# Dilated heads of a hybrid encoder layer: the first and last query block share a unit with 192 keys each

## The chip, the core and the metric

The kernel runs on one core of a Trainium2 chip. The metric is the device time of one execution in microseconds (us), as the median of several. Engines are named as in the profile: PE is the matrix engine (PEld its loading of the stationary operand), DVE the vector engine, ACT the scalar engine, POOL GpSimd, SP the engine that issues most DMAs.

## The reference

One encoder layer on 1024 tokens of width 1024 in float32: a feed-forward half step, a mixing step with 16 attention heads of width 64, and a second feed-forward half step. Eight heads (group B) mix three dilated windows; this case is about them.

```python
DIL_PATTERNS = ((128, 1), (512, 4), (2048, 16))
...
def dilated_window_attention(q, k, v, t5_bias, window, dilation):
    radius = window // (2 * dilation)
    ...
    off = k_pos[:, None, :] - q_pos[:, :, None]
    valid = (jnp.abs(off) <= radius) & (k_pos[:, None, :] >= 0) & (k_pos[:, None, :] < L)
    bias = t5_bias[:, t5_bucket(off * dilation)].astype(jnp.float32)
    s = jnp.einsum('bhdnqe,bhdnke->bhdnqk', qs, k_blk) * HEAD_DIM ** -0.5
    s = jnp.where(valid, s + bias[:, None], MASK_VALUE)
    m = jnp.max(s, axis=-1, keepdims=True)
    p = jnp.exp(s - m)
    den = jnp.sum(p, axis=-1)
    o = jnp.einsum('bhdnqk,bhdnke->bhdnqe', p, v_blk) / den[..., None]
    lse = m[..., 0] + jnp.log(den)
    ...
def dilated_mixture_attention(q, k, v, t5_bias):
    results = [dilated_window_attention(q, k, v, t5_bias, w, d) for w, d in DIL_PATTERNS]
    wts = jax.nn.softmax(lses, axis=0)
    return jnp.sum(wts[..., None] * outs, axis=0).astype(q.dtype)
```

For the pattern (128, 1), the local one, a query sees the keys at most 64 tokens away. A block of 128 queries in the middle of the sequence so sees 256 keys; the first block (tokens 0 to 127) and the last (896 to 1023) see 192, since there are no tokens beyond the ends.

## The kernel before, in words

The feed-forward steps and the projections come first (to about 890 us), then the eight dilated heads (about 890 to 1012 us), then the eight neighbourhood heads (`na_head`, to about 1120 us), the output projection and the second feed-forward step.

The dilated heads are taken in pairs (class `DilPair`, p = 4 to 7), two heads of 64 columns side by side. A head is 8 units, each with two query blocks: four units for the local part (`part` 0) and four for the dilated part (`part` 1), in two quads of two units. `head` runs the dilated quads first, then the local ones; in the very first head it is the other way round, and its first local quad is begun earlier, among the last products of the projection (`begin`).

A unit goes through these steps. PE makes the scores of each of the two blocks in two products (L1163; the stationary operand is the queries in the tile `st`, the moving one the keys, split into a high and a low part, so two products add up in PSUM). DVE adds the bias and takes the row maximum (`softmax_rows`, L1070), ACT takes the exponential and the row sum (L1072) and writes it in another order of keys. PE transposes the result in blocks of 128 keys (`transpose_blocks`, L1080), ACT or DVE copies it out of PSUM (L1082), and PE multiplies by the values (`outs`, L1184). After two units, one copy brings four blocks of output from PSUM to SBUF (L1192). The values of the local part lie in the tile `va` in slots of 128 tokens, shifted by 64 so that slots blk - 1 and blk serve block blk; the first and the last block have two slots of their own (7, 8 and 9, 10), and their 256 keys are clamped to the ends (`k0`, 0 and 768).

The steps are pipelined by hand: `Ctx.unit` queues a unit's transposes and value products and emits those of three and of four units earlier, so PE sees scores, transposes and value products of three different units in turn. The order is fixed as written for the engines within `ordered`; DMA issues and some POOL work are tied to places by `behind` and `queued`. `next_ready` converts the queries and reorders a bias table on POOL (L1059) for the next head; `merge` joins the patterns after a pair, with two products on POOL (L1237, L1238). Loads of the next heads go through SP (`va` L1100, `vb` L1098, keys L1052, bias L1112) and POOL (queries L1050). In the last two pairs, a quarter of a weight tile is split on ACT and DVE (L127, L128) once per quad.

Of the kernel before, what the change touches and what calls it, by code (L numbers as in the profile page):

```python
# [18 lines left out]
SEQ, D, DFF = 1024, 1024, 2816  # L19
P, T = 128, 512  # L20
# [1054 lines left out]
def transpose_blocks(c, src, n, eng):  # L1075

    nc = c.nc
    ps = c.pst.tile([P, 4, P], F32, tag="tr", name="ptp")
    for j in range(n):
        nc.tensor.transpose(ps[:, j, :], src[:, j * P:(j + 1) * P], c.ident)  # L1080
    pt = c.ptp.tile([P, 4, P], F32, tag="pt", name="pt")
    (nc.scalar.copy if eng else nc.vector.tensor_copy)(pt[:, :n], ps[:, :n])  # L1082
    return pt


class DilPair:


    def __init__(self, c, p, then):

        self.c, self.p, self.pi, self.then = c, p, p - NP, then
        nc, pi = c.nc, self.pi
        vp = c.vp[p % 2]
        self.va = vp.tile([P, 11, P], F32, tag="va", name="va", bufs=1)
        self.vb = vp.tile([P, 4, 2, P], F32, tag="vb", name="vb", bufs=1)
        v = c.v[1][:, pi * P:(pi + 1) * P]
        for j in range(2):
            nc.sync.dma_start(self.vb[:, :, j], v[j * T:j * T + T].rearrange("(i c) f -> i c f", c=4))  # L1098
        for u0, n, t0 in ((0, 7, 64), (7, 2, 0), (9, 2, 768)):
            nc.sync.dma_start(self.va[:, u0:u0 + n], v[t0:t0 + n * P].rearrange("(u t) f -> t u f", t=P))  # L1100

    def outputs(self):
        c = self.c
        self.oa = c.op.tile([P, 8, P], F32, tag="oa", name="oa")
        if self.pi:
            self.sa = c.op.tile([P, 8, 4], F32, tag="sa", name="sa")
        self.ob = c.op.tile([P, 8, RW], F32, tag="ob", name="ob")
# [20 lines left out]
    def quad(self, hd, st, q, g, part, quad, first=False, mid=()):  # L1128
        c, nc = self.c, self.c.nc
        po = []  # L1130
        by_c, g0 = st.rearrange("p q (c t) -> p q c t", c=4), g[:, 0].rearrange("p (c t) -> p c t", c=4)
        for un in range(2):
            if mid and un == mid[1]:
                c.behind(mid[0].popleft(), DVE, ACT)
            if first:
                ps, s, pb = [x.rearrange("p (a b) -> p a b", a=2) for x in (
                    c.psm.tile([P, T], F32, tag="mm", name="sp"), c.sp.tile([P, T], F32, tag="s1", name="s"),
                    c.next_pb())]
            else:
                ps = c.pss.tile([P, 2, 256], F32, tag="s", name="sp")  # L1140
                s = c.pp.tile([P, 2, 256], F32, tag="s", name="s")
                pb = s if part else c.next_pb().rearrange("p (a b) -> p a b", a=2)
            todo = []
            for j in range(2):
                blk = quad * 4 + un * 2 + j
                out, sj = ps[:, j], s[:, j]
                ex = pj = sj
                if part:
                    ci, jh = blk // 2, blk % 2
                    lhs = q[:, blk * P:(blk + 1) * P]  # L1150
                    keys = [st[:, i, ci * 256:(ci + 1) * 256] for i in (1, 2)]
                    bias = g[:, 1, 128 - 128 * jh:384 - 128 * jh]
                else:
                    k0 = min(max(blk * P - 64, 0), 768)
                    lhs = st[:, 0, blk * P:(blk + 1) * P]
                    keys = [by_c[:, i, :, k0 // 4:k0 // 4 + 64] for i in (1, 2)]
                    x0 = k0 - blk * P + 128
                    bias = g0[:, :, x0 // 4:x0 // 4 + 64]
                    ex = sj.rearrange("p (c u t) -> p u c t", c=4, u=2)
                    pj = pb[:, j].rearrange("p (u t c) -> p u c t", u=2, c=4)  # L1160
                    out, sj = [x.rearrange("p (c t) -> p c t", c=4) for x in (out, sj)]
                for i in range(2):
                    nc.tensor.matmul(out, lhs, keys[i], start=i == 0, stop=i == 1)  # L1163
                stt, o0 = (self.ob, P) if part else (self.sa, 0)
                at = blk % 2 * 4 + blk // 2 if part else blk
                todo.append((out, bias, sj, ex, pj, stt[:, at, o0 + hd:o0 + hd + 1],
                             stt[:, at, o0 + 2 + hd:o0 + 3 + hd]))
            for args in todo:
                softmax_rows(c, *args)
            pt, on_act = [], un if part else not (un or quad or first)  # L1170
            c.unit(lambda s=pb, un=un, pt=pt, on_act=on_act: pt.append(
                       transpose_blocks(c, s.rearrange("p a b -> p (a b)"), 4, on_act)),
                   lambda un=un, pt=pt: self.outs(hd, part, quad, un, pt[0], po))

    def outs(self, hd, part, quad, un, pt, po):
        c, nc = self.c, self.c.nc
        if un == 0:
            po.append(c.pso.tile([P, 4, P], F32, tag="o", name="po"))
        po = po[0]
        for j in range(2):  # L1180
            blk = quad * 4 + un * 2 + j
            for t in range(2):
                rhs = self.vb[:, blk // 2, t, :] if part else self.va[:, {0: 7, 7: 9}.get(blk, blk - 1) + t, :]
                nc.tensor.matmul(po[:, un * 2 + j], pt[:, 2 * j + t, :], rhs, start=t == 0, stop=t == 1)  # L1184
        if un == 0:
            return
        f = slice(hd * 64, hd * 64 + 64)
        to, got = self.oa[:, quad * 4:quad * 4 + 4, f], po[:, :, f]
        if part:
            to = self.ob.rearrange("p (j c) w -> p c j w", j=2)[:, 2 * quad:2 * quad + 2, :, f]  # L1190
            got = got.rearrange("p (c j) w -> p c j w", j=2)
        (nc.scalar.copy if quad else nc.vector.tensor_copy)(to, got)  # L1192
        if hd and part:
            self.regroup(quad)
        c.tick()
        if (hd, part, quad) == (1, 0, 1):
            c.todo.extend([lambda: None] + [lambda: c.behind(self.merge, DVE, ACT)])
# [67 lines left out]
def na_head(c, p, hd, og, vs, st, nb, late, done):  # L1265
    nc = c.nc
    kv = [st[:, 1 + i].rearrange("p (r w) -> p r w", r=16) for i in range(2)]
    for s in range(8):
# [24 lines left out]
        def outs(s=s, u=u, k0=k0, n=n, pt=pt, stt=stt, po=po):  # L1293
# [720 lines left out]
```

## Time and profile before

| what | value |
|---|---|
| median of 3 runs | 1832.79 us (1831.18 to 1834.72) |
| profiled execution, its span (the only time that the page gives for it) | 1831.5 us |
| PE busy | 1814.0 us, 99% of the span, 8904 matmuls |
| loading of stationary operands (PEld) | 1526.9 us, 83% |
| DVE, ACT, POOL busy | 1321.9, 835.6, 322.5 us |
| chain that ended last | PE 80%, issue 11%, DMA 3%, DVE 3%, ACT 2%, POOL 1% |

A matmul's busy time is its own duration, and several are under way at once, so busy time on PE is more than the time that PE's work takes; the steps between starts, as the chain shows them, tell what one costs. A float32 value product is recorded as two matmuls, a score product (in the rounded kind, F32R) and a transpose as one.

### The profile page before, as it was taken

How to read it: one execution, taken by the hardware profiler on the slowest of the kernel's cores; microseconds unless marked ns; L12 is line 12 of the kernel's file. 1: busy time of each engine (PE TensorE's matmuls, PEld its weight loads, DVE VectorE, ACT ScalarE, POOL GpSimd, SP SyncE). 2: the span in 40 equal slices, each digit the busy share in tenths (PEclk: the TensorE clock that was granted, in tenths of full speed). 3: DMA queues.
4: the chain of work that ended last, by engine and by line, in shares of the span. 5: the costliest groups of instructions: out<-in, count | busy, mean ns of one | idle time of the engine just before them, and what ended most of it. 6: DMA issues, size and time to landing. Idle time of an engine off the chain costs nothing.

```text
span 1831.5 us, 25146 instructions
## 1 busy us (share of the span) xinstructions
PE 1814.0 (99%) x8904; PEld 1526.9 (83%) x8904; DVE 1321.9 (72%) x2251; ACT 835.6 (46%) x1487; POOL 322.5 (18%) x508
## 2 busy tenths in 40 slices
PE   8999999999999999999999999999999999999998
PEld 6887888888888888888899998888888888888886
DVE  6878876776466877477778866788887777654557
ACT  6622233334443657134688765564223333354433
POOL 2223211112021123132332100121111111110000
PEclk9999999999999999999999999999999999999999
DMA  7756565557888867869686533594555566596564
GB/s 276 260 186 209 163 235 213 212 201 254 307 302 309 280 207 257 271 221 300 199 275 220 196 112 105 183 319 171 187 175 207 191 223 224 184 349 201 189 229 147
DMA packets 172992, 409.67 MB, mean 224 GB/s; under 512 B 20081, under 2 KB 42513, under 8 KB 170818
## 3 DMA queue, kind: packets, MB, share of 16 engines
q1 hardware_dynamic: 124706, 246.33, 40.8%
q0 software_dynamic: 47152, 159.64, 24.0%
q10 hardware_dynamic: 1008, 2.10, 0.3%
q8 instruction: 70, 1.15, 0.3%
q14 instruction: 56, 0.46, 0.1%
HBM read 280.49 MB, written 132.56 MB: 226 GB/s over the span
## 4 chain that ended last, share of the span: by engine, by line
PE 80%; issue 11%; DMA 3%; DVE 3%; ACT 2%; POOL 1%; SPq 0%; POOLq 0%; DVEq 0%; ACTq 0%
PE accp L783 24%; PE mmp L466 14%; PE mmp L467 14%; PE mmp L472 14%; PE po L1184 3%; PE ptp L1080 2%; PE po L1297 2%; PE accp L357 1%; PE accp L359 1%; PE accp L358 1%; PE sp L1163 1%; PE trp L174 1%; PE sp L1281 1%; POOL g L717 1%; ACT pb L1072 1%
## 5 line engine op out<-in xcount | busy, mean ns | idle before, releaser
L466 PE MATMUL mmp<-x,whi 128*128 128x512 f32 (+1 forms) x1464 | 571.8, 391 | 1.6 <-ACT x L181 1.4
L467 PE MATMUL mmp<-x,whi 128*128 128x512 f32 (+1 forms) x1464 | 569.3, 389 | 0.7 <-DVE x L182 0.6
L783 PE MATMUL accp<-pw 128*128 128x512 f32 x1800 | 411.2, 390 | 0.3 <-ACT hb L804 0.3
L783 PEld LDWEIGHTS accp<-pw 128*128 128x128 f32 x1800 | 337.2, 188 | 70.5 <-ACT hb L804 0.7
L472 PE MATMUL mmp<-x,wlo 128*128 128x512 f32 (+1 forms) x1464 | 390.6, 389 | 0.0
L466 PEld LDWEIGHTS mmp<-x,whi 128*128 128x128 f32 x1464 | 275.9, 188 | 59.9 <-ACT x L181 2.0
L467 PEld LDWEIGHTS mmp<-x,whi 128*128 128x128 f32 x1464 | 275.9, 188 | 57.5 <-DVE x L182 1.5
L472 PEld LDWEIGHTS mmp<-x,wlo 128*128 128x128 f32 x1464 | 274.8, 188 | 56.7
L751 DVE TENSOR_TENSOR pw<-praw,pw 128x1024 fp32r<-128x1024 f32 (+1 forms) x181 | 199.6, 1141 | 127.4 <-ACT pw L750 126.7
L750 ACT CAST pw<-praw 128x1024 fp32r<-128x1024 f32 (+1 forms) x181 | 168.4, 983 | 207.1 <-PE accp L783 163.8
L456 ACT CAST whi<-wraw 128x1024 fp32r<-128x1024 f32 x126 | 132.7, 1053 | 186.1 <-PE mmp L467 160.8
L457 DVE TENSOR_TENSOR wlo<-wraw,whi 128x1024 fp32r<-128x1024 f32 x126 | 153.1, 1217 | 2.3 <-ACT whi L456 2.3
L693 POOL DMA_DIRECT2D g<-sg x44 | 24.0, 545 | 432.3 <-DVE sg L686 242.9
L481 ACT COPY s<-mmp 128x512 f32<-128x512 f32 x52 | 30.7, 590 | 132.3 <-PE mmp L472 121.6
L456 ACT CAST whi<-traw 128x512 fp32r<-128x512 f32 x52 | 32.3, 621 | 125.5 <-DVE traw L554 96.4
L645 DVE TENSOR_TENSOR c<-mmp,u 128x512 f32<-128x512 f32 x52 | 35.9, 691 | 70.1 <-PE mmp L472 69.7
L553 DVE TENSOR_TENSOR wraw<-wraw 128x1024 f32<-128x1024 f32 x52 | 63.6, 1224 | 18.5 <-DMA wraw<-in_wu_dram 17.8
L783 PE MATMUL accp<-pw,x 128*128 128x512 f32 x312 | 71.8, 390 | 0.0
L783 PEld LDWEIGHTS accp<-pw,x 128*128 128x128 f32 x312 | 58.3, 188 | 12.3 <-DVE pw L751 0.4
L632 DVE TENSOR_TENSOR c<-mmp,v 128x512 f32<-128x512 f32 x52 | 35.8, 689 | 34.1 <-PE mmp L472 34.1
L1297 PE MATMUL po<-vs,pt 128*128 128x128 f32 x352 | 49.9, 276 | 0.0
L1080 PE MATMUL ptp<-ident,pb 128*128 128x128 f32 x304 | 48.8, 272 | 0.0
(273 smaller groups left out, 2491.4 us busy)
## 6 DMA issues: line engine op xcount, KB each, us to landing
praw<-g SPq DMA_DIRECT2D x70, 512.0 KB, 5.6
wraw<-in_wg_dram SPq DMA_DIRECT2D x44, 512.0 KB, 4.2
wraw<-in_wu_dram SPq DMA_DIRECT2D x44, 512.0 KB, 7.1
tr<-in_wd_dram SPq DMA_DIRECT2D x44, 512.0 KB, 6.3
g<-sg POOLq DMA_DIRECT2D x88, 256.0 KB, 5.4
ts<-tr POOLq DMA_DIRECT2D x22, 1024.0 KB, 4.7
praw<-ts SPq DMA_DIRECT2D x88, 256.0 KB, 3.9
praw<-in_wd_dram SPq DMA_DIRECT2D x66, 256.0 KB, 5.7
```

The costliest lines, as they stand in the source:

```text
L456: nc.scalar.copy(hi, raw)
L457: nc.vector.tensor_sub(lo, raw, hi.bitcast(F32))
L466: mm(out, hi[:, i, sl], xhi[:, k, cols], start=not go_on and k == 0, stop=False, skip_group_check=go_on)
L467: mm(out, hi[:, i, sl], xlo[:, k, cols], start=False, stop=False, skip_group_check=go_on)
L472: mm(out, lo[:, i, sl], xhi[:, k, cols], start=False, stop=k == 3, skip_group_check=go_on)
L553: nc.vector.tensor_sub(r[:, 0:2], r[:, 1:3], r[:, 0:2])
L750: nc.scalar.copy(hi, raw[:, :m])
L751: nc.vector.tensor_sub(lo, raw[:, :m], hi.bitcast(F32))
L783: c.nc.tensor.matmul(acc[t], a, b, start=not chained and gi == 0 and j == i == 0, stop=end and j + n >= len(ops) and i == len(two) - 1, sk ...
L1080: nc.tensor.transpose(ps[:, j, :], src[:, j * P:(j + 1) * P], c.ident)
L1184: nc.tensor.matmul(po[:, un * 2 + j], pt[:, 2 * j + t, :], rhs, start=t == 0, stop=t == 1)
L1297: nc.tensor.matmul(po[0][:, u], pt[0][:, j, :], vs[:, k0 + j, :], start=j == 0, stop=j == n - 1)
```

## The change

Blocks 0 and 7 form a unit of their own, the first one of the second local quad; the other blocks are regrouped: (1, 2) and (5, 6) in the first quad, (0, 7) and (3, 4) in the second. In the edge unit each block has its 192 keys alone, so scores, bias, maximum and exponential run over 2 x 192 columns instead of 2 x 256, and the 384 columns make three transposes. The middle one holds the last 64 keys of block 0 and the first 64 keys of block 7. It is multiplied by two slots of values at once (8 and 9), of which each has 64 tokens and zeros in the other half of the partitions, into the output of both blocks; the other two transposes have a product each. The three products write only the 64 columns of the head at hand. The value tile is loaded with five DMAs instead of three, and POOL clears the two halves that no DMA writes.

```diff
@@ DilPair.__init__
-        for u0, n, t0 in ((0, 7, 64), (7, 2, 0), (9, 2, 768)):
+        for u0, n, t0 in ((0, 7, 64), (7, 1, 0), (10, 1, SEQ - P)):
             nc.sync.dma_start(self.va[:, u0:u0 + n], v[t0:t0 + n * P].rearrange("(u t) f -> t u f", t=P))
+        for j, t0 in enumerate((P, SEQ - P - 64)):
+            nc.gpsimd.memset(self.va[64 - 64 * j:P - 64 * j, 8 + j], 0.0)
+            nc.sync.dma_start(self.va[64 * j:64 * j + 64, 8 + j], v[t0:t0 + 64])
@@ DilPair.quad
+        edge = not part and quad
...
-            todo = []
-            for j in range(2):
-                blk = quad * 4 + un * 2 + j
+            todo, m = [], 256
+            if edge and un == 0:
+                m = 192
+                ps, s, pb = [x.rearrange("p a b -> p (a b)")[:, :2 * m].rearrange("p (a b) -> p a b", a=2)
+                             for x in (ps, s, pb)]
+            for j, blk in enumerate(self.blocks(part, quad, un)):
...
-                    k0 = min(max(blk * P - 64, 0), 768)
+                    k0 = max(blk * P - 64, 0)
                     lhs = st[:, 0, blk * P:(blk + 1) * P]
-                    keys = [by_c[:, i, :, k0 // 4:k0 // 4 + 64] for i in (1, 2)]
+                    keys = [by_c[:, i, :, k0 // 4:(k0 + m) // 4] for i in (1, 2)]
                     x0 = k0 - blk * P + 128
-                    bias = g0[:, :, x0 // 4:x0 // 4 + 64]
+                    bias = g0[:, :, x0 // 4:(x0 + m) // 4]
...
-            c.unit(lambda s=pb, un=un, pt=pt, on_act=on_act: pt.append(
-                       transpose_blocks(c, s.rearrange("p a b -> p (a b)"), 4, on_act)),
+            c.unit(lambda s=pb, un=un, pt=pt, on_act=on_act, n=m // 64: pt.append(
+                       transpose_blocks(c, s.rearrange("p a b -> p (a b)"), n, on_act)),
                    lambda un=un, pt=pt: self.outs(hd, part, quad, un, pt[0], po))
+
+    def blocks(self, part, quad, un):
+        return ((quad * 4 + un * 2, quad * 4 + un * 2 + 1) if part else
+                (((1, 2), (5, 6)), ((0, 7), (3, 4)))[quad][un])
@@ DilPair.outs
-        po = po[0]
-        for j in range(2):
-            blk = quad * 4 + un * 2 + j
-            for t in range(2):
-                rhs = self.vb[:, blk // 2, t, :] if part else self.va[:, {0: 7, 7: 9}.get(blk, blk - 1) + t, :]
-                nc.tensor.matmul(po[:, un * 2 + j], pt[:, 2 * j + t, :], rhs, start=t == 0, stop=t == 1)
+        po, f = po[0], slice(hd * 64, hd * 64 + 64)
+        if not part and (quad, un) == (1, 0):
+            nc.tensor.matmul(po[:, 0:4:3, f], pt[:, 1, :], self.va[:, 8:10, f], start=True, stop=False,
+                             skip_group_check=True)
+            for j in range(2):
+                nc.tensor.matmul(po[:, 3 * j, f], pt[:, 2 * j, :], self.va[:, 7 + 3 * j, f], start=False, stop=True,
+                                 skip_group_check=True)
+        else:
+            for j, blk in enumerate(self.blocks(part, quad, un)):
+                o = 1 + j if quad and not part else un * 2 + j
+                for t in range(2):
+                    rhs = self.vb[:, blk // 2, t, :] if part else self.va[:, blk - 1 + t, :]
+                    nc.tensor.matmul(po[:, o], pt[:, 2 * j + t, :], rhs, start=t == 0, stop=t == 1)
...
-        to, got = self.oa[:, quad * 4:quad * 4 + 4, f], po[:, :, f]
+        got = po[:, :, f]
...
+        else:
+            to = self.oa.rearrange("p (a b) w -> p a b w", a=2)[:, :, 0:4:3, f]
+            if not quad:
+                to = self.oa.rearrange("p (a b) w -> p a b w", a=2)[:, :, 1:3, f]
+            got = got.rearrange("p (a b) w -> p a b w", a=2)
```

On PE, at the second local quad of the very first head, these rows stood before (`sp` are scores, `ptp` transposes, `po` value products; `pb` and `pt` belong to local units here, and `st,q` marks the scores of the dilated part that follows):

```order
L1163 MATMUL sp<-st 128x256 x8
L1080 MATMUL ptp<-ident,pb 128x128 x4
L1163 MATMUL sp<-st,q 128x256 x4
L1080 MATMUL ptp<-ident,pb 128x128 x4
L1184 MATMUL po<-va,pt 128x128 x4
L1163 MATMUL sp<-st,q 128x256 x4
L1080 MATMUL ptp<-ident,pb 128x128 x4
L1184 MATMUL po<-va,pt 128x128 x4
L1163 MATMUL sp<-st,q 128x256 x4
L1080 MATMUL ptp<-ident,pb 128x128 x4
L1184 MATMUL po<-va,pt 128x128 x4
```

And these stand there now:

```order
L1170 MATMUL sp<-st 128x192 x4
L1170 MATMUL sp<-st 128x256 x4
L1080 MATMUL ptp<-ident,pb 128x128 x4
L1170 MATMUL sp<-st,q 128x256 x4
L1080 MATMUL ptp<-ident,pb 128x128 x4
L1202 MATMUL po<-va,pt 128x128 x4
L1170 MATMUL sp<-st,q 128x256 x4
L1080 MATMUL ptp<-ident,pb 128x128 x3
L1202 MATMUL po<-va,pt 128x128 x4
L1170 MATMUL sp<-st,q 128x256 x4
L1080 MATMUL ptp<-ident,pb 128x128 x4
L1192 MATMUL po<-va,pt 128x2x64
L1195 MATMUL po<-va,pt 128x64 x2
```

The order of the units is the same; the edge unit's scores have become narrower, and one transpose and one value product are gone.

On POOL, the piece between the query loads of the third pair's two heads (`st<-qk_0_86`) reads, with - for before and + for now:

```order
 L1050 DMA st<-qk_0_86 128x1024
-L1059 COPY g<-g 128x384
-L1059 COPY q<-st 128x1024
+L1059 COPY q<-st 128x1024
+L1059 COPY g<-g 128x384
+L1102 MEMSET va 64x128 x2
 L1050 DMA st<-qk_0_86 128x1024
```

The two memsets stand ahead of the load of the second head's queries, and the conversion of the queries has moved ahead of the reordering of the bias.

On SP, the loads of the second pair (`va`, and `st<-qk_1_85` for its keys) and what follows them:

```order
 L1100 DMA va<-v_95 128x7x128
 L1052 DMA st<-qk_1_85 128x1x2048
-L1100 DMA va<-v_95 128x2x128 x2
-L1112 DMA g<-gab 128x2x384
-L1202 DMA rg_90<-ob 128x2x264
+L1100 DMA va<-v_95 128x128 x2
+L1103 DMA va<-v_95 64x128 x2
+L1115 DMA g<-gab 128x2x384
+L1224 DMA rg_90<-ob 128x2x264
 L1052 DMA st<-qk_1_87 128x1x2048
```

Two more issues stand ahead of the bias load and the output store; the order is otherwise the same.

More of the change, by code (lines that the diff above doesn't have):

```diff
@@ L1178, in outs @@
             po.append(c.pso.tile([P, 4, P], F32, tag="o", name="po"))
-        po = po[0]
-        for j in range(2):
-            blk = quad * 4 + un * 2 + j
-            for t in range(2):
-                rhs = self.vb[:, blk // 2, t, :] if part else self.va[:, {0: 7, 7: 9}.get(blk, blk - 1) + t, :]
-                nc.tensor.matmul(po[:, un * 2 + j], pt[:, 2 * j + t, :], rhs, start=t == 0, stop=t == 1)
+        po, f = po[0], slice(hd * 64, hd * 64 + 64)
[11 more added lines that the diff above has]
+                    nc.tensor.matmul(po[:, o], pt[:, 2 * j + t, :], rhs, start=t == 0, stop=t == 1)
         if un == 0:
             return
-        f = slice(hd * 64, hd * 64 + 64)
-        to, got = self.oa[:, quad * 4:quad * 4 + 4, f], po[:, :, f]
+        got = po[:, :, f]
         if part:
```

## The prediction

> **What bounds the kernel now.** I read the page first, then the stretches around the dilated heads, then the chain that ended last through them, then the groups of instructions there with shapes kept apart, and last the waits and the DMA queues.
>
> ```profile
> span 1831.5 us, 25146 instructions
> PE 1814.0 (99%) x8904; PEld 1526.9 (83%) x8904; DVE 1321.9 (72%) x2251; ACT 835.6 (46%) x1487; POOL 322.5 (18%) x508
> PEclk9999999999999999999999999999999999999999
> ```
>
> PE is busy for 99% of the span at an undisturbed clock. Busy time overlaps, though (each matmul is pipelined), so it does not say that PE is the limit at one given place. The stretches through the dilated heads say more:
>
> ```profile
> core 0: us, PE busy (x) PEld busy (x) DVE busy (x) ACT busy (x) POOL busy (x), PEclk, DMA share, GB/s
> 900.00:910.00 10.00, 10.00 (x91) 10.00 (x90) 6.91 (x29) 7.93 (x28) 2.35 (x2) 1.00 1.00 309
> 910.00:920.00 10.00, 10.00 (x91) 10.00 (x91) 6.08 (x25) 9.02 (x29) 3.49 (x3) 1.00 0.41 125
> 960.00:970.00 10.00, 9.79 (x86) 9.53 (x86) 8.55 (x39) 7.90 (x29) 4.96 (x4) 1.00 0.69 251
> 970.00:980.00 10.00, 9.88 (x87) 9.64 (x87) 7.27 (x29) 9.22 (x30) 3.05 (x3) 1.00 0.51 158
> ```
>
> In an undisturbed stretch 91 matmuls start in 10 us; at 960 to 980 only 86 or 87 do. So PE sets the pace of the dilated heads, with losses of about half a microsecond in a few places; ScalarE (ACT) is at 90% where a local part runs (910 to 920). The chain gives the price of each kind of PE work (start, duration, what, count):
>
> ```profile
> 889.15 0.91 PE mmp L472 x4
> 904.88 0.48 PE sp L1163 x4
> 905.36 0.44 PE ptp L1080 x4
> 905.80 0.89 PE po L1184 x8
> 906.69 0.48 PE sp L1163 x4
> 1005.88 0.24 PE sp L1281 x2
> 1007.45 0.36 PE sp L1281 x2
> ```
>
> One unit of two query blocks is four score products (L1163, 256 columns, 0.48 us, so 0.12 each), four transposes (L1080, 0.44, so 0.11 each) and four value products, which the chip records as eight passes (L1184, 0.89, so 0.111 a pass and 0.223 a product). Period: 0.48 + 0.44 + 0.89 = 1.81 us (904.88 to 906.69). The rows of L1281 are the neighbourhood heads' scores, 256 columns at 0.12 and 384 at 0.18; L472 has 512 columns at 0.228. Wide products go by the column. No row here is below 0.11, whatever it does.
>
> **The change on PE.** The edge unit occurs once per head, eight times in all. It loses one transpose: 0.11 us. It loses one value product, two passes: 0.223. Both are on the path. That is 0.333 a unit, certain as far as PE is the limit.
>
> Two prices are not in this trace, since nothing narrower than 128 columns, and no score product narrower than 256, runs. (a) The four score products have 192 columns. The line through 256 and 384 (0.12 and 0.18) gives 0.09 at 192; the shortest step of any kind is 0.11; nothing excludes the other side, and the dearest neighbour per column is the value product, 0.223 for 128, which gives 0.334 at 192. I take 0.11, because two different kinds (transpose and value pass) both stand there: 4 x 0.01 = 0.04 gained. (b) Two of the three value products have 64 columns, four passes in all. By the column they would take 0.056 a pass; as they stand now, 0.111. I take 0.111, the same floor, so nothing gained. The third product writes two runs of 64 into PSUM; local and dilated scores, which read their keys in four runs and in one, bound what cutting a row into runs costs:
>
> ```profile
> L1163 PE MATMUL sp<-st,q 128*128 128x256 f32 x128 | 23.1, 302 | 0.0
> L1163 PE MATMUL sp<-st 128*128 128x256 f32 x128 | 22.4, 299 | 0.0
> ```
>
> The first group holds the dilated scores (one run), the second the local ones (four runs); they differ by 3 ns, so I put the runs at nothing.
>
> The Trainium skill, "TensorE: Matmul & The Clock Gate", section "LDWEIGHTS (loading the stationary operand)", says that loading 128 stationary columns takes 128/1.2 = 107 ns however little is streamed; by that the scores would give 4 x 0.013 and my sum would be 3.1 us. The transposes at 0.11 agree with it, though they do not prove it. The same page, "Back-to-back issue gap", prices an isolated product by columns alone (192 columns at 82 ns); that is the first rival's rule, and the transposes here, at 110 ns for 128 columns where it has 56, speak against it.
>
> Sum on PE: 0.11 + 0.223 + 0.04 = 0.373 a unit, times 8 = 3.0 us.
>
> **What the other engines do with it.** A stall that stood behind PE could eat this. In the groups (mean ns of one after the busy time):
>
> ```profile
> L1072 ACT ACTIVATE pb<-s,sa 128x256 f32<-128x256 f32 x64 | 43.2, 757 | 1.0 <-DVE sa L1070 0.7
> L1072 ACT ACTIVATE pb<-sb,stt 128x384 f32<-128x384 f32 x48 | 29.5, 616 | 17.9 <-DVE stt L1070 16.2 <-DVE y L159 0.6 <-DVE dn L1222 0.6
> L1072 ACT ACTIVATE pb<-sb,stt 128x256 f32<-128x256 f32 x16 | 8.2, 510 | 3.3 <-DVE stt L1070 3.3
> L1070 DVE CUSTOM_DVE_ANT_0 sb<-sp,nb 128x384 f32<-128x384 f32 x48 | 26.6, 555 | 21.8 <-PE sp L1281 21.5
> L1070 DVE CUSTOM_DVE_ANT_1 s<-sp,g 128x256 f32<-128x256 f32 x64 | 24.6, 421 | 12.3 <-PE sp L1163 10.4 <-ACT oa L1192 1.0 <-ACT ob L1192 0.4
> L1082 DVE COPY pt<-ptp 128x512 f32<-128x512 f32 x41 | 28.1, 686 | 0.0
> L1082 DVE COPY pt<-ptp 128x384 f32<-128x384 f32 x24 | 13.3, 554 | 1.2 <-PE ptp L1080 1.2
> ```
>
> VectorE (DVE): from 384 to 256 columns the row maximum loses 134 ns, so to 192 about 67, twice; the copy out of PSUM goes from 686 to 554. DVE saves 0.13 + 0.13 = 0.27 us a unit. ACT: two exponentials, each between 53 ns shorter (half of 616 - 510) and 189 ns shorter (a quarter of 757): 0.1 to 0.38 us a unit. Both get lighter by about as much as PE does. In the last four heads (two pairs) the weight splits share ACT and DVE, and there PE already waits:
>
> ```profile
> 955.61 2.50 ACT pb L1072 x8
> 963.70 0.43 DVE wlo L128
> 964.98 0.61 DVE pt L1082
> 965.73 1.13 PE po L1184 x8
> ```
>
> The value passes at 965.73 wait for a copy that DVE did late behind ACT's exponentials and a split. The edge unit is the second last of a head (in all but the first), so ACT's 0.1 to 0.38 saved there helps against the same backlog; I leave that stall as it is. The output copies keep their 256 elements, in another order of blocks, and the first quad takes blocks 1, 2, 5, 6 at the old prices: nothing.
>
> **Loads and memsets.** Five DMAs for the value tile instead of three, and two GpSimd (POOL) memsets, per pair. SP waits, and POOL waits and a memset of a similar size:
>
> ```profile
> SPq L1202 <- DVE ob L1192: 45.1, 4, 12.6
> POOL g L1059 <- DMA g<-gab: 33.7, 5, 11.1
> 902.36 1.11 SPq L1100 DMA_DIRECT2D va<-v  x2
> masks.py:197 POOL MEMSET ident<- 128x128 f32 x1 | 0.2, 205 | 0.3 <-POOLq L2004 0.3
> 926.43 2.08 POOL L1059 CAST q<-st 128x1024 fp32r<-128x1024 f32 x1
> 930.96 0.53 POOL L1050 DMA_DIRECT2D st<-qk  x1 [2.44 <-PE sp L1163]
> ```
>
> Two more issues at about 0.55 us each stand on SP ahead of the next bias and output stores, where SP then waits 45 us in all for outputs: covered; uncovered they would cost 1.1 us a pair. The memsets, 0.2 each or less, are 1.6 us on an engine that waits 33.7 for biases. In the third and fourth pair they wait for PE's last read of the tile two pairs back; behind them are queued the load of the next queries (L1050) and, behind that, the merge products. POOL stood idle 2.44 us at that very place (928.5 to 930.96), waiting for PE too, so the wait fits; uncovered, it would delay a load that PE needs one head later. The cast and the bias copy change places: the cast is wanted first, and no row shows PE waiting for either.
>
> After the heads the program moves as a block: its last piece on the chain is unbroken PE work.
>
> ```profile
> 1614.45 209.51 PE accp L783 x924
> ```
>
> So 3.0 us come off the profiled execution: span 1831.5 to 1828.5. The page lists for it only the span; the median of the three runs is 1832.8, 1.3 above it, so 1832.8 - 3.0 = **1829.8 us**.
>
> **The rivals.** *One: narrow steps really are cheap.* Scores at 0.09 and four passes at 0.056 give 0.333 + 0.12 + 0.22 = 0.67 a unit, 5.4 us if all of it stays. In the four heads with splits ACT gives back only up to 0.38, so 4 x 0.67 + 4 x 0.38 = 4.2: 1827.4 to 1828.6, middle 1828.0. For: wide products go by the column. Against: the 0.11 floor of every 128-column step. *Two, slower: a score product below 256 columns falls to the pace of the value products.* All score products here read the F32R tile `st` with 256 columns or more, so the trace can't deny it. Price: 0.334 - 0.12 = 0.214, times 4 = 0.857, less 0.333: +0.52 a unit, +4.2 us, 1837.0. It decides from 0.12 + 0.333/4 = 0.203 us a product on. Against: 256, 384 and 512 columns lie on a line with no step on the way. *Three: hidden.* In the four heads with splits ACT sets the pace and saves 0.1 a unit: 4 x 0.373 + 4 x 0.1 = 1.9 us, 1830.9. For: ACT at 9.22 of 10 at 970 to 980. Against: 87 of 91 matmuls still start there. That the change does not do what it says is excluded by the order of the instructions, which shows three transposes and three products in the edge units.
>
> **How the numbers follow.** 0.2% is 3.7 us, about what a measurement of this kernel can tell from no change. The forecast has 0.52; its own range, 8 x 0.333 = 2.7 to 8 x 0.453 = 3.6 (scores at 0.09) with about a microsecond of scatter of medians (the three runs lie 3.5 apart), is 1828.2 to 1831.1; since 3.0 is close to the limit, 0.19 of the 0.52 goes to faster, 0.33 to same. Rival one has 0.23, 0.22 of it faster and 0.01 same. Rival two has 0.15, 0.13 slower and 0.02 same. Rival three has 0.10, all same. Faster 0.41, same 0.46, slower 0.13. The range runs from 1827.0 (rival one less half a microsecond) to 1832.5 (rival three and scatter); it leaves out the slower rival and a little at the ends.
>
> **What would show it.** In the changed profile's chain the edge unit should read: four scores at 0.44 instead of 0.48, three transposes at 0.33, six passes at 0.67, period 1.44 instead of 1.81. Scores of 0.36 or passes of 0.06 mean rival one; scores above 0.8 for four mean rival two. Unchanged PE periods with waits for ACT around 955 to 995 mean rival three. A new wait of the load of queries (L1050) on POOL, or of PE for the value tile, would make the working wrong in its covered terms.

## The result, and the profile after

| kernel | median of 21 runs, us | profiled execution, span |
|---|---|---|
| before | 1832.88 (1831.18 to 1835.31) | 1831.5 |
| changed | 1835.87 (1834.16 to 1837.80) | 1834.9 |

The ratio is 1.0016, with a 95% interval of 1.0009 to 1.0022: the change costs 3.0 us where 3.0 us less was forecast. The 1835.87 lies outside the range given (1827.0 to 1832.5).

The saving on PE is there. The chain through one local part of the changed kernel, about 980 us (start, duration, what, count):

```profile
979.61 0.48 PE sp L1170 x4
980.09 0.33 PE ptp L1080 x3
980.41 0.89 PE po L1202 x8
981.31 0.48 PE sp L1170 x4
981.79 0.44 PE ptp L1080 x4
982.23 0.22 PE po L1192 x2
982.45 0.39 PE po L1195 x4
982.84 0.53 PE sp L1170 x4
```

Three transposes take 0.33 where four took 0.44, and the edge unit's six passes 0.22 + 0.39 = 0.61 where eight took 0.89. Of these 0.28 us 0.05 are given back at once: the four scores behind the edge unit's passes take 0.53, the others 0.48. So the two missing passes are worth 0.23, and the whole edge unit about what was forecast. But the stretches through the last four heads, read as in the prediction, have lost matmuls:

```profile
core 0: us, PE busy (x) PEld busy (x) DVE busy (x) ACT busy (x) POOL busy (x), PEclk, DMA share, GB/s
950.00:960.00 10.00, 8.76 (x74) 8.14 (x74) 8.86 (x32) 7.69 (x26) 4.64 (x5) 1.00 0.92 262
960.00:970.00 10.00, 9.80 (x86) 9.46 (x85) 7.76 (x33) 7.76 (x28) 3.95 (x2) 1.00 0.58 216
970.00:980.00 10.00, 8.29 (x71) 7.82 (x71) 6.73 (x21) 7.62 (x26) 3.50 (x3) 1.00 0.43 139
```

The first of these stretches reads, in the kernel before:

```profile
950.00:960.00 10.00, 10.00 (x90) 9.93 (x89) 9.29 (x31) 8.53 (x28) 3.33 (x3) 1.00 0.99 298
```

74 matmuls start where 90 did, and 71 where 87 did (970 to 980), at a full clock (1.00). From 955 to 985 us DVE, ACT and POOL are all less busy than before (23.23, 23.45 and 8.38 us against 25.11, 25.66 and 11.06): an order or a wait, not work. Who waits for whom from 950 to 1010 us (total, times, longest; the rows on exponentials behind row maxima, on copies out of PSUM and on splits), changed kernel first, then before:

```profile
ACT pb L1072 <- DVE sa L1070: 5.1, 5, 2.1
PEld po L1202 <- ACT pt L1082: 3.8, 4, 1.3
PE po L1202 <- ACT pt L1082: 2.9, 4, 1.1
PEld po L1202 <- DVE pt L1082: 2.7, 4, 1.5
PE po L1202 <- DVE pt L1082: 1.6, 3, 1.3
DVE wlo L128 <- ACT whi L127: 1.3, 3, 0.6
```

```profile
ACT pb L1072 <- DVE sa L1070: 0.7, 2, 0.5
PE po L1184 <- DVE pt L1082: 0.4, 2, 0.2
PEld po L1184 <- DVE pt L1082: 0.4, 1, 0.4
DVE wlo L128 <- ACT whi L127: 0.2, 1, 0.2
```

ACT waits for DVE's row maxima, and PE for copies out of PSUM on both engines: 2.9 + 1.6 = 4.5 us, where it waited 0.4. One such place in full, the edge unit of the fifth head, in order of time (in brackets the idle time before, and who ended it):

```profile
956.98 0.41 ACT L127 CAST whi<-wraw 128x256 fp32r<-128x256 f32 x1
957.42 0.42 DVE L128 TENSOR_TENSOR wlo<-wraw,whi 128x256 fp32r<-128x256 f32 x1 [0.57 <-ACT whi L127]
957.76 0.35 DVE L1070 CUSTOM_DVE_ANT_1 s<-sp,g 128x192 f32<-128x192 f32 x1
958.15 0.64 ACT L1072 ACTIVATE pb<-s,sa 128x192 f32<-128x192 f32 x1 [0.77 <-DVE sa L1070]
958.65 0.62 ACT L1072 ACTIVATE pb<-s,sa 128x192 f32<-128x192 f32 x1
959.14 1.04 ACT L1082 COPY pt<-ptp 128x512 f32<-128x512 f32 x2
959.75 0.94 PE L1202 MATMUL po<-vb,pt 128*128 128x128 f32 x6 [1.11 <-ACT pt L1082]
```

ACT's copy `pt` belongs to the last dilated unit, three units earlier; its transposes were done. It stands behind the edge unit's two exponentials, these wait for DVE's row maximum, that one for the split L128, and that for ACT's own half of the split, L127. PE stands 1.11 us at the end of the row. In the kernel before, at the same place, the copy runs straight behind the split and the exponentials follow:

```profile
957.97 0.39 ACT L127 CAST whi<-wraw 128x256 fp32r<-128x256 f32 x1
958.33 0.59 ACT L1082 COPY pt<-ptp 128x512 f32<-128x512 f32 x1
958.81 0.76 ACT L1072 ACTIVATE pb<-s,sa 128x256 f32<-128x256 f32 x1
959.42 0.76 ACT L1072 ACTIVATE pb<-s,sa 128x256 f32<-128x256 f32 x1
960.19 0.59 ACT L1082 COPY pt<-ptp 128x512 f32<-128x512 f32 x1
```

No line of the diff moves that copy. ACT's instructions at this head in the two built programs, before on the left:

```
L127 CAST whi<-wraw 128x256                    L127 CAST whi<-wraw 128x256
L1082 COPY pt<-ptp 128x512                     L1072 ACTIVATE pb,sa<-s,sa 128x2x4x24 x2
L1072 ACTIVATE pb,sa<-s,sa 128x2x4x32 x2       L1082 COPY pt<-ptp 128x512 x2
L1082 COPY pt<-ptp 128x512                     L1072 ACTIVATE pb,sa<-s,sa 128x2x4x32 x2
L1072 ACTIVATE pb,sa<-s,sa 128x2x4x32 x2
```

This corrects a sentence of mine further up ("The order is fixed as written for the engines within `ordered`"): that holds for PE alone. ACT, DVE and POOL are put in order by a scheduler, and shorter edge rows made it put the exponentials first, in seven of the eight heads. On DVE it moved four splits (two in the first head of the third and of the fourth pair), on POOL the cast of the queries ahead of the bias copy of the head before.

The second place is 971 us. The changed kernel, the split against POOL's cast:

```profile
971.06 0.42 DVE L1070 CUSTOM_DVE_ANT_1 s<-sp,g 128x256 f32<-128x256 f32 x1
971.11 2.08 POOL L1059 CAST q<-st 128x1024 fp32r<-128x1024 f32 x1
971.48 1.99 DVE L128 TENSOR_TENSOR wlo<-wraw,whi 128x256 fp32r<-128x256 f32 x1
973.39 0.68 DVE L1082 COPY pt<-ptp 128x512 f32<-128x512 f32 x1
974.12 0.49 PE L1202 MATMUL po<-vb,pt 128*128 128x128 f32 x2 [1.25 <-DVE pt L1082]
```

A split of 0.42 us took 1.99: it began under the cast and ended 0.28 us after it (971.11 + 2.08 = 973.19; 971.48 + 1.99 = 973.47). The row maximum, which reads PSUM, ran beside the cast at its usual 0.42. PE paid 1.25 us.

### The profile page after: what moved, and what is told of

Its sections match the earlier page's. It is cut to its first block, busy times and chain, and to the rows that moved or that the text cites. A ratio compares the mean times of both kernels' runs of the same rounds, so it can differ in the third digit from the quotient of the medians.

```text
span 1834.9 us, 25124 instructions
## 1 busy us (share of the span) xinstructions
PE 1813.2 (99%) x8880; PEld 1523.0 (83%) x8880; DVE 1320.7 (72%) x2251; ACT 833.5 (45%) x1487; POOL 324.0 (18%) x516
## 4 chain that ended last, share of the span: by engine, by line
PE 60%; issue 29%; DVE 4%; POOL 3%; ACT 2%; DMA 1%; POOLq 0%; DVEq 0%; SPq 0%; ACTq 0%
PE accp L783 16%; PE mmp L467 10%; PE mmp L466 10%; PE mmp L472 10%; PE po L1202 2%; PE po L1319 2%; PE ptp L1080 2%; PE accp L357 1%; PE accp L359 1%; PE accp L358 1%; POOL g L717 1%; PE sp L1303 1%; PE trp L174 1%; PE sp L1170 1%; ACT pb L1072 1%
```

## The experiments

The ratios here, mostly of medians of 11 runs (7 for b_act, 6 for zero_all), have intervals of plus or minus 1.6 to 2.2 us. The stretch ahead of the dilated heads varies by up to 4 us from one profile to the next (they begin between 891.4 and 895.5). So each profile was also read by the dilated heads alone, from PE's first score product of the second local quad of the very first head (its first quad is begun earlier) to the first one of the neighbourhood heads. For before and changed, the first and the last row, in that order:

```profile
893.58 1.10 PE L1163 MATMUL sp<-st 128*128 128x256 f32 x8
1005.63 0.48 PE L1281 MATMUL sp<-st 128*128 128x256 f32 x2
```

```profile
892.81 1.08 PE L1170 MATMUL sp<-st 128*128 128x192 f32 x8
1008.30 0.49 PE L1303 MATMUL sp<-st 128*128 128x256 f32 x2
```

For zero_all these starts are 893.52 and 1001.15, for every_second 893.74 and 1002.50, for before_second_four 893.31 and 1005.12. The table has the difference, and in the same way the eight heads, each from its first score product to the next head's. The first is short, since its first quad is left out. An edge unit's transposes and products come three and four units after its scores, so the second head's lie in the third, and the last head's, 0.33 us of saving, behind the end of this measure. Ratios are against runs of the kernel before on the same chip, taken together with each kernel's own.

| kernel | heads 1 to 8, us | sum | median | ratio, 95% interval |
|---|---|---|---|---|
| before | 9.25 14.45 14.45 14.45 14.56 15.36 14.54 14.98 | 112.05 | 1832.88 | |
| changed | 8.79 14.57 14.24 14.25 16.01 16.90 15.18 15.55 | 115.49 | 1835.87 | 1.0016 [1.0009, 1.0022] |
| x_act | 8.79 14.40 14.07 14.07 14.37 15.75 14.23 14.85 | 110.53 | 1832.45 | 0.9998 [0.9989, 1.0007] |
| x_pool | 8.79 14.57 14.25 14.25 15.49 15.57 15.19 15.56 | 113.65 | 1834.82 | 1.0010 [1.0001, 1.0019] |
| x_all | 8.79 14.40 14.07 14.07 14.50 16.48 14.48 14.87 | 111.66 | 1832.02 | 0.9994 [0.9985, 1.0003] |
| b_act | 9.25 14.94 14.93 14.95 15.15 16.19 15.12 16.19 | 116.73 | 1838.10 | 1.0027 [1.0017, 1.0038] |
| zero_before | 9.26 14.45 14.45 14.45 14.45 14.45 14.45 14.45 | 110.42 | 1831.69 | 0.9993 [0.9984, 1.0001] |
| zero_after | 8.79 14.57 14.24 14.25 14.25 14.25 14.25 14.24 | 108.82 | 1830.18 | 0.9985 [0.9976, 0.9994] |
| zero_all | 8.79 14.40 14.07 14.07 14.07 14.07 14.07 14.08 | 107.63 | 1827.78 | 0.9968 [0.9956, 0.9980] |
| x_best | 8.81 14.40 14.07 14.07 14.49 15.64 14.78 14.86 | 111.13 | 1832.12 | 0.9993 [0.9984, 1.0002] |
| cast_in_four | 8.79 14.40 14.07 14.21 14.49 15.21 14.49 14.87 | 110.54 | 1831.40 | 0.9994 [0.9985, 1.0003] |
| every_second | 8.79 14.40 14.07 14.07 14.07 14.69 14.08 14.58 | 108.76 | 1829.81 | 0.9980 [0.9971, 0.9989] |
| every_first | 8.81 14.40 14.07 14.45 14.44 14.93 14.46 14.94 | 110.49 | 1832.49 | 0.9996 [0.9987, 1.0004] |
| before_second | 9.25 14.45 14.45 14.45 14.45 16.76 14.45 15.02 | 113.30 | 1833.91 | 1.0002 [0.9993, 1.0011] |
| before_second_four | 9.25 14.46 14.45 14.45 14.45 15.26 14.45 15.03 | 111.81 | 1833.49 | 1.0003 [0.9994, 1.0012] |

**x_act: ScalarE's order alone.** `softmax_rows` is split in two, `which` choosing the row maximum or the exponential:

```diff
+            late = edge and un == 0 and len(c.units) >= 3
             for args in todo:
-                softmax_rows(c, *args)
+                softmax_rows(c, *args, which=(1, 0) if late else (1, 1))
...
+            if late:
+                c.behind(lambda: [softmax_rows(c, *args, which=(0, 1)) for args in todo], ACT)
```

> The changed kernel, with one thing put back: in the second local quad of a head ScalarE again takes the copy of the last dilated unit ahead of the edge unit's two exponentials (behind them in the changed kernel, in seven of eight heads). VectorE's and GpSimd's order stays that of the changed kernel. Theory A (the loss is ScalarE's order: PE waits for a copy that stands behind exponentials, which wait for the split): about 4.4 us of 1835.9 go, 1831.5, or 0.9993 of the kernel before; the waits of PE for the copy at L1082 around 958, 990 and 1006 go. Theory B (the loss is GpSimd's cast running into VectorE's split): 1835.9, within 0.3. Theory C (PE got lighter and ScalarE and VectorE now set the pace, in whatever order): 1835.9, and the waits only move.

The median falls by 3.4 us, the dilated heads by 115.49 - 110.53 = 4.96. In the profile of x_act PE waits nowhere long for ACT's copy; from 950 to 1006 us its longest waits for copies are DVE's:

```profile
ACT pb L1074 <- DVE sa L1071: 1.7, 5, 0.5
PEld po L1207 <- DVE pt L1084: 1.6, 4, 0.4
PE po L1207 <- DVE pt L1084: 0.5, 3, 0.2
```

Theory A holds as the larger part, and theory C, that nothing but the work counts, falls.

**b_act: the same order on the kernel before.** In the second local quad the copy is put behind the first unit's exponentials, and the second unit's exponentials behind the next copy.

```diff
         if len(self.units) >= 4:
-            self.units[-4][0]()
+            if last:
+                self.behind(self.units[-4][0], ACT)
+            else:
+                self.units[-4][0]()
+        if then:
+            self.behind(then, ACT)
...
```

> The kernel before, with ScalarE's order of the changed kernel: the copy of the last dilated unit behind the two exponentials of the first unit of the second local quad; the work is that of before. Theory A: the loss comes without the change, 3.5 to 4.5 us: 1836.4 to 1837.4, ratio 1.0019 to 1.0025, with PE waiting for the copy at L1082 in the last four dilated heads. Theories B and C: 1832.9, ratio 1.0000, since GpSimd's order and PE's work are those of before.

1838.1, 5.1 us above before and more than A expected: the heads without splits lose as well, 14.94 for 14.45, where wider exponentials stand ahead of the copy. The order needs no narrow unit to do its harm. (A few of DVE's row maxima behind the joining of the patterns also changed places here.)

**x_pool: GpSimd's order alone.** The cast is tied behind the bias copy that the call before made:

```diff
+                        with ExitStack() as es:
+                            for i in tied:
+                                es.enter_context(tc.issue_after(i))
-                        qs.append(q_by_residue(c, nc.gpsimd.tensor_copy, st))
+                            qs.append(q_by_residue(c, nc.gpsimd.tensor_copy, st))
...
```

> The changed kernel, with GpSimd's order alone put back: the cast of a head's queries stands again behind the copy of the bias of the head before. Theory B: the split at 971 us falls from 1.99 us to its usual 0.43 and the output copy at 952 from 2.22 to 1.22, PE's stall of 1.4 us at 972 shrinks to the 0.4 that it was before: 1.4 us in all, 1834.5. Theory A: the stalls behind ScalarE's exponentials stay, 1835.4 to 1835.9. Theory C: 1835.9.

1834.8, a microsecond less (within the interval), and 1.84 less in the dilated heads, 1.33 of it in the sixth head, where the collision was. B holds as the smaller part.

**x_all: everything back in its old order.** x_act and x_pool, and the four splits on DVE.

> The changed kernel with the order of before on ScalarE, GpSimd and VectorE (there the weight split stands again between the edge unit's two row maxima, and ahead of the first row max of the second dilated quad, in the first head of the third and fourth pair). The work is that of the changed kernel, the order that of before. Theories A and B together: the whole saving of the edge units on PE remains, 8 x 0.38 = 3.0 us below the kernel before: 1829.8, ratio 0.9984. Theory C: 1835.9, or at most 1 us less; if ScalarE's pace in the four heads with splits is the limit, as the third rival of the prediction had it, 1830.9.

1832.0: not the 1829.8 that A and B foretold. Its first four heads have the saving (14.07 for 14.45), its sixth has 16.48. The same collision came back, though the order was that of before; POOL's start depends on a load:

```profile
967.28 0.90 POOL L1062 COPY g<-g 128x384 f32<-128x384 f32 x1 [2.33 <-DMA g<-gab]
968.11 2.08 POOL L1062 CAST q<-st 128x1024 fp32r<-128x1024 f32 x1
968.41 2.06 DVE L131 TENSOR_TENSOR wlo<-wraw,whi 128x256 fp32r<-128x256 f32 x1
```

And the other heads with splits gain nothing or 0.1 us. So a theory D came up, the prediction's third rival: in heads with splits the other two engines set the pace.

**Without the splits, first attempt.** Three kernels leave the 16 quarter splits out and copy the raw tile by DMA instead.

> The kernel before, without the splits of the four weight tiles in the last four dilated heads (16 quarter splits on ScalarE and VectorE are left out; the raw tile is copied by DMA into both halves). Theory D (the four heads with splits are paced by ScalarE and VectorE, the others by PE): the last four heads fall from 15.0 us, as they measure now, to the 14.45 of the first four: about 1.6 us less than the kernel before, 1831.4. Theory A alone (only the order matters, and before's order costs nothing): 1833.0, no change.

> The changed kernel without those splits; ScalarE's order is still that of the changed kernel. Theory D with A (the late copy costs much only where a split stands in the queue): all eight heads take 14.24 us, as the first four do in the changed kernel: 8 x 0.21 = 1.7 us below the same kernel of before without splits, about 1829.7, and some 6 us below the changed kernel. Theory A in a form without the splits (copies behind exponentials cost their 4.4 us wherever they stand): 1834 or more. Theory C (lighter PE is paced by the other two everywhere): as the kernel of before without splits, 1831.4.

> The changed kernel without those splits, with ScalarE's and GpSimd's order of before. Theory D: all eight heads take 14.06 us, as the first four do with that order: 8 x 0.39 = 3.1 us below the kernel of before without splits, about 1828.3: the whole forecast saving, where nothing else works beside it. Theory C: less than 1 us below that kernel, 1830.5 or more.

They gave 1833.9, 1831.6 and 1834.8, ratios 1.0005 [0.9996, 1.0014], 0.9993 [0.9984, 1.0002] and 1.0009 [1.0000, 1.0017], and settle nothing: DVE now stood waiting for the load of `obn` (ns_all, 955 to 1000 us), which SP issued 3.0 us later than before (956.29 for 953.31), behind other issues that now include the copies:

```profile
DVE mn L1254 <- DMA obn<-rg: 8.5, 2, 4.3
```

**Without the splits, second attempt.** The half tiles are cleared by POOL long before, and nothing stands in the splits' place; the weights of one projection are thus zeros.

> The kernel before, without the 16 quarter splits of weights in the last four dilated heads and without any DMA in their place: the eight half tiles are cleared once by GpSimd in the second pair. Theory D (heads with splits are paced by ScalarE and VectorE): every head takes 14.45 us, 110.4 from the first dilated scores to the first neighbourhood scores against 112.05, so about 1.6 us off the kernel before, 1831.3. If the splits cost PE nothing: 1833.0.

> The changed kernel without those splits, ScalarE's order as in the changed kernel. Theory D with A: 14.24 us a head, 108.8 for the dilated heads, 1.9 us below the kernel of before without splits, about 1829.4, and six below the changed kernel. Theory C: as the kernel of before without splits.

> The changed kernel without those splits, with ScalarE's and GpSimd's order of before. Theory D: 14.07 us a head, 107.6 for the dilated heads, and 0.33 more in the first neighbourhood head, where the last edge unit's transposes and products lie: 3.0 us below the kernel of before without splits, about 1828.2, and its interval apart from that kernel's. Theory C: less than 1 us below it.

The sums are 110.42, 108.82 and 107.63 against 110.4, 108.8 and 107.6 expected. Every head of zero_all takes 14.07 to 14.08 from the third on. Without the splits the change is worth 2.79 us here and 0.33 behind it, 3.1 in all, and the medians differ by 3.9 with their intervals just apart. D holds as far as this: the loss is there only with the splits. Without them even the changed kernel with its own order (zero_after) is 1.6 us shorter in these heads than zero_before. Whether the splits' work costs it or their place in the queues of ACT and DVE is left to the last runs.

**x_best: one split moved out of the cast's way.** As x_all, with the sixth head's third split one unit earlier.

> The changed kernel with the order of before on ScalarE, VectorE and GpSimd, and in the second head of the third pair the third quarter split one unit earlier, where VectorE waits 0.9 us for PE and GpSimd's cast of the queries has not begun. Theory B (a VectorE split that begins under the cast is held to its end: 2.06 us instead of 0.43, and PE 1.47 in the run with this order): 1.4 us below that run's profile in this head, 1831 by the median, 0.9990 of the kernel before. If the earlier split holds ScalarE's copy by its 0.39 instead, the gain is 1.1 us. If the collision is an accident of single executions, no change: 1832.

1832.1, no gain to be told from x_all. The split, now at 967.79, met the cast again, which began at 967.75 in this execution, and took 2.31 us. Its premise, that the cast would not have begun, was wrong: the cast's start moves with the load.

**cast_in_four.** As x_all, with the cast in four pieces:

```diff
-    by_residue(copy, q, st[:, 0])
+    to, x = q.rearrange("p (r t) -> p r t", r=4), st[:, 0].rearrange("p (t r) -> p r t", r=4)
+    for i in range(0, 4, 4 // parts):
+        copy(to[:, i:i + 4 // parts], x[:, i:i + 4 // parts])
```

> The changed kernel with the order of before on ScalarE, VectorE and GpSimd, and the cast of the queries (1024 columns in one instruction of 2.1 us) as four of 256 columns, about 0.55 us each. Theory B (a VectorE operation with two inputs in SBUF that begins under the cast is held until the instruction ends): no split is held longer than a piece, 0.43 + 0.55 = 1.0 us at most where it was 2.06, and the sixth head falls from 16.5 to about 15.3 us: 1.1 us off that run, 1830.9. If VectorE is held for as long as GpSimd works at all: still 2 us, and no change, 1832.0.

The same split, begun under the last piece, takes 0.80 where it took 2.06:

```profile
969.55 0.80 DVE L131 TENSOR_TENSOR wlo<-wraw,whi 128x256 fp32r<-128x256 f32 x1
```

The sixth head falls from 16.48 to 15.21, as expected. That the hold lasts to the end of an instruction, and not for as long as POOL works, this row can't tell, since no piece follows; every_second (below) shows it, where a split begins under the third of four pieces:

```profile
969.52 0.66 POOL L1066 CAST q<-st 128x256 fp32r<-128x256 f32 x1
969.85 0.61 DVE L128 TENSOR_TENSOR wlo<-wraw,whi 128x256 fp32r<-128x256 f32 x1
970.12 0.86 POOL L1066 CAST q<-st 128x256 fp32r<-128x256 f32 x1
```

It ends 0.28 us behind its piece (970.46 and 970.18), in the middle of the next. The median moved by 0.6, within its interval.

**Where the splits stand.** On cast_in_four's arrangement (without the ties on DVE), the splits go to the second unit of each quad, or to the first.

```diff
-                self.quad(hd, st, q, g, part, quad, mid=(more, (i + 1) % 2) if more else ())
+                self.quad(hd, st, q, g, part, quad, mid=(more, 1) if more else ())
```

> The changed kernel with the order of before on ScalarE (edge unit) and GpSimd and the cast in four pieces, and with the quarter splits in the second unit of each quad (units 2, 4, 6, 8 of a head) where they were in units 2, 3, 6, 7. Theory E (the 2.8 us that the splits cost here come from two splits in neighbouring units, whose copies PE then waits 0.3 us for): the dilated heads fall from 110.5 to about 109, the time to 1829.8. Theory D alone (ScalarE's and VectorE's work as such is too much for the four heads, wherever the splits stand): 110.5 and 1831.4.

> The same with the splits in the first unit of each quad (1, 3, 5, 7), where they stand ahead of the exponentials. Theory E: as with the second unit, about 109 and 1829.8. Theory D alone: 110.5. If it is the place ahead of the edge unit's exponentials that costs, and not the neighbour: 110 or more here and 109 there.

> The kernel before with its splits in the second unit of each quad; nothing else is changed. If the places of the splits cost the same in both kernels (1.6 us at most here, since that is all that leaving them out gave): 111 for the dilated heads where it was 112.05, 1832. If they cost only where PE's work is shorter: 112, 1833.

every_second gives 1829.8, ratio 0.9980 [0.9971, 0.9989], and 108.76 us: faster than both kernels, and the forecast of 1829.8 is reached, though by another arrangement than the one it was made for. Heads five and seven take 14.07 and 14.08, as if there were no splits. Theory E as I put it, neighbouring splits, falls with every_first, which has no neighbours either and stays at 110.5. That is also what was expected if the place ahead of the edge unit's exponentials costs, but the trace of every_first shows the loss elsewhere. In its heads five and seven the edge unit and the one behind it take 1.76 and 1.80 us from their first score product to the next unit's, as without splits (zero_all: 1.76 and 1.81), and 0.33 us are lost in the head's second unit (2.03 for 1.70). There, in the fifth head, the split stands ahead of a copy out of PSUM:

```profile
945.77 0.39 ACT L127 CAST whi<-wraw 128x256 fp32r<-128x256 f32 x1
946.20 0.42 DVE L128 TENSOR_TENSOR wlo<-wraw,whi 128x256 fp32r<-128x256 f32 x1 [0.20 <-ACT whi L127]
946.54 0.68 DVE L1086 COPY pt<-ptp 128x512 f32<-128x512 f32 x1
947.27 0.63 PEld L1209 LDWEIGHTS po<-va,pt 128*128 128x128 f32 x5 [0.30 <-DVE pt L1086]
```

In every_second the same copy runs ahead of the split (946.63 and 947.98), and PE does not wait. So in these two heads it is the place ahead of a copy that PE waits for that costs. (every_first's fourth head, without a split, takes 14.45 because the same copy came late for another reason: DVE had stood 1.25 us waiting for the load of `obn`, 0.83 in every_second.) before_second has 14.45 in the fifth and seventh head, but a split of 2.34 us under the cast in the sixth. So the control was made once more with the cast in four.

> The kernel before with the splits in the second unit of each quad and the cast in four pieces: the same arrangement as the best variant of the changed kernel, with the work of before. If that arrangement alone makes the gain: as that variant, 1829.8, ratio 0.9980. If the edge unit's work makes it (Theory D with E: 14.45 us for heads five and seven, about 15.1 for six and eight): 111.3 us for the dilated heads against 108.76 there, that is 0.7 us below the kernel before, 1832.2, and 2.5 + 0.33 us above the variant.

1833.5 and 111.81, where 1832.2 and 111.3 were expected: the arrangement alone gives the kernel before nothing that can be measured. Between these two lie 111.81 - 108.76 = 3.05 us and the 0.33 behind them. They run ACT in the same order, and POOL too but for the memsets, but not DVE, which was left to the scheduler: in every_second four splits stand one row maximum earlier, and two later. The work accounts for 2.79 of the 3.05; the other 0.26 may be DVE's order.

## Why the prediction was wrong, by its own steps

**Right: the sum on PE.** 0.373 a unit, 3.0 us, was forecast. The kernels without splits show 0.38 a head (14.45 to 14.07), 3.1 in all. Rivals one (steps by the column) and two (narrow products fall back) are false. The four 64-column passes take 0.39, not 0.22, and 0.05 more in the scores behind them, so 0.44 as priced. Of the second head's edge unit only the four scores lie in that head, and it went from 14.45 to 14.40: 0.0125 a product, so 0.107 for 192 columns, neither 0.09 nor 0.334. The loads and memsets cost PE nothing, as forecast: from 890 to 1010 us all its waits in the changed kernel are for copies out of PSUM.

**Wrong: "I leave that stall as it is".** This step failed. Splits cost 110.42 to 112.05, 1.63 us, in the kernel before, but 108.82 to 115.49, 6.67, in the changed one. I priced ACT and DVE by durations, found both lighter, and took their order as given. I had looked at the order on PE, POOL and SP, and not on the two engines that the stall was known to stand on. There the runs showed, in place of a stall that stays as it is, a copy behind the wrong instructions: with ACT's order alone put back (x_act), 4.96 us of the dilated heads' 115.49 go.

**Wrong: "The cast and the bias copy change places ... no row shows PE waiting for either".** PE does not wait for the cast; DVE does, about 1.6 us at a time (1.99 for 0.42), and PE for DVE. The row that could have warned was in the trace of before, 6 us behind the wait that I called a stall, in the same head. A split took 0.91 there, under a cast that began at 970.37 and ended at 972.45:

```profile
971.83 0.91 DVE L128 TENSOR_TENSOR wlo<-wraw,whi 128x256 fp32r<-128x256 f32 x1
```

**Rival three** (1.9 us less) named the right place. With before's order, x_act and cast_in_four gain 112.05 - 110.53 = 1.5 and 0.33 behind, 1.85 us, near its 1.9. Its reason, that ACT sets the pace of the four heads, does not hold, though: in every_second, with the same work, heads five and seven give the whole saving (14.07 and 14.08 for 14.45), and only six and eight fall short of it (14.69 and 14.58).

**Luck.** The largest of the three chances, 0.46, lay on "same", and 1.0016 is within the 0.2% that the prediction calls no change. It was given for a gain too small to tell, not for 3.0 us lost, so nothing in the working earned it.

**The account** in the dilated heads: work -2.79 (zero_all to zero_before), order without splits +1.19 (zero_after to zero_all), splits +5.04 (6.67 - 1.63): together +3.44, which is 115.49 - 112.05. Put back one at a time, ACT's order takes back 4.96 (x_act) and POOL's 1.84 (x_pool), but all three orders together only 3.83 (x_all), since a split met the cast again there: these do not add up, and a collision's cost depends on what else is late. What DVE's four moved splits are worth by themselves was not separated, and one profile per kernel does not tell how often the cast and a split meet.

## What to carry to other kernels

When a change alters durations in a program that a scheduler orders, compare the order on every engine that is known to stall, not only on the one that is shortened: here the copies behind the wrong instructions cost more than the edit saved. Price a saving per stage with the other engines' side work left out (16 small splits here), and it shows at once whether the work or the queue is at fault. Then move the side work behind what the critical engine waits for: here that, with the copies put back and the cast cut in four, turned 3.0 us lost into 3.2 us gained (1829.8 against 1833.0 on the same chip).

## What the runs showed of the hardware

A VectorE instruction with two inputs in SBUF that begins under a GpSimd cast waits for the end of that instruction; a split of 256 columns ends about 0.28 us behind it: 1.99 and 2.06 for 0.42, and 0.80 under pieces a quarter as long; row maxima and copies that read PSUM ran beside it at their usual 0.42 and 0.68. Another operation with two inputs in SBUF, the product `og` of the changed kernel, took 2.22 where it usually takes 1.22 (it began at 951.96 under the cast of 951.00). The Trainium skill, "SBUF — State Buffer", section "SBUF: two separate sides", says of such waits: the two engines share a pair of ports, and an operation with two SBUF inputs and a GpSimd operation that reads SBUF lock each other out for a whole instruction. The traces agree, in the lengths above; the 0.28 us are this case's own.

Cutting a cast of 1024 columns in four costs GpSimd about 0.4 us: pieces of 0.65 to 0.67 us that overlap a little, 2.45 from the first's start to the last's end (cast_in_four, from 967.62) against 2.08.
